# Three pieces of a recurrence's element-wise work change engine: GpSimd's subtractions to VectorE, its copies to ScalarE

## The chip, the cores and the metric

The kernel runs on one core of a Trainium2 chip. The time is the device time of one execution in microseconds (us), the median of three runs. Engines are named as in the profile: PE is TensorE (its weight loads are PEld), DVE is VectorE, ACT is ScalarE, POOL is GpSimd, and SP is the engine that issues the transfers.

## The reference, cut to what matters

One decoder layer over 1024 tokens of width 1024, in float32:

```
h  = rmsnorm(x);  u = h @ w_in            # 1024 x 5376, split into the parts below
oA = RWKV7(u[:, :1792])                   # 8 heads of 64, state 64x64, one step per token
oB = DiffAttention(u[:, 1792:3328])       # 4 heads, two softmax maps each
x += (sig(gA) * (oA @ PA) + sig(gB) * (oB @ PB)) @ w_out
x += relu(rmsnorm(x) @ W1)^2 @ W2
x += (p @ w_ple) * sig(rmsnorm(x) @ w_ple_gate)
out = rmsnorm(x)

S_t = S_{t-1} diag(w_t) + (S_{t-1} a_t) b_t^T + v_t k_t^T ;  y_t = S_t r_t
y   = groupnorm(y) * lnx_w + lnx_b ;  oA = (y + bonus) * g
```

## The kernel before, in words

Every large product is made from three products of split operands: a value is stored as `hi` (its rounding to a shorter format) and `lo` (what the rounding left), and `mm3` (L155 to L160) adds hi·hi (L158), hi·lo (L159) and lo·hi (L160). So each weight tile needs one cast for `hi` (ACT, L151) and one subtraction for `lo` (L152). `weights` (L143) issues the transfer of the raw tile on SP (L148), the cast, and the subtraction on POOL or DVE, by its argument `lo`.

The first phase, 40 to 700 us, holds the projection with `w_in` and the recurrence together. The projection is a generator, `stream`: 42 jobs of 128 output columns, each two halves of 24 matmuls of 512 columns, and each `next(stream)` issues three matmuls. Raw weights have one buffer, hi and lo two each, so the cast of job n+1 waits until PE has finished with job n-1, and the transfer of a raw tile waits until the subtraction before it has read the buffer. The halves land in two PSUM buffers (`pd`) and are emptied by `spill` (L330 to L347) or `mixed` (L305 to L311), on ACT and DVE.

The recurrence runs in four passes of two heads (`rwkv`). A pass prepares decays, keys and bonus (L403 to L471, on ACT, DVE and PE; `vs` is the value tile with the two 64-token halves of each block swapped, L460); forms small triangular matrices (L496 to L510); inverts them on DVE in 31 dependent steps of two instructions (L525, L526), with transfers through DRAM before (`dr_blk`) and after (`dr_inv`, `XS`); and then runs 18 ticks in which units of 128 tokens are built (L618 to L645) and the state is carried forward (L605 on PE, L609 on DVE). A group norm over four units runs beside the ticks (L585 to L597, with POOL's power of -1/2 at L107), and `post` forms the branch's output `of`, its hi part (L670) and its lo part (L671), and stores both. Between these steps the passes call `next(stream)` a fixed number of times, so that PE has projection work while the other engines work on the chain.

Each engine takes its instructions in one fixed order. That order is written when the kernel is built, by a planner that goes through the program in order of priority and places what it expects to be ready; so it is near the order of the text, not the same (L378 stands before L375 on DVE). An instruction that waits holds all that is behind it on its engine. On SP, transfers are issued in the same manner.

Of the kernel before, what the change touches and what calls it, by code (L numbers as in the profile page):

```python
# [10 lines left out]
F32R = mybir.dt.float32r  # L11
BF16 = mybir.dt.bfloat16
AF = mybir.ActivationFunctionType
ALU = mybir.AluOpType
# [4 lines left out]
P = 128  # L19
# [3 lines left out]
KD = D // P  # L23
# [56 lines left out]
class Kern:  # L80
# [82 lines left out]
    def run(self):  # L163
        nc, tc, A = self.nc, self.tc, self.A
        with ExitStack() as es:
# [24 lines left out]
            with ExitStack() as right:  # L190
                mA = self.phase_a2(opener, right, a1r, stream)
                front.close()
                mid = ExitStack()
                self.f1w = opener(mid)("f1w", 5)

                hb = opener(mid)("hb", 1)
                self.hb = {i: [hb.tile([P, 4, H], F32R, name=f"hb{i}{n}") for n in ("hi", "lo")] for i in (0, 1)}
                self.h2 = opener(mid)("h2", 1).tile([P, KD, T], F32, name="h2")
                with ExitStack() as e:
                    self.out_proj(opener(e), mA)  # L200
# [12 lines left out]
    def phase_a1(self, pool, rpool):  # L213
# [16 lines left out]
        with tc.tile_pool(name="a1n", bufs=2) as nw:  # L230
            def scale(j):

                sq = nw.tile([P, D], BF16, tag="sq", name="sq")
                ss = nw.tile([P, 1], F32, tag="nrm_ss", name="nrm_ss")
                nc.scalar.activation(sq, xs[j], AF.Square, accum_out=ss)
                r = self.rstd(nw, ss, 1, 1.0 / D, NORM_EPS)
                d = nw.tile([P, P], F32, tag="diag", name="diag")
                nc.vector.tensor_scalar(d, self.cst("ident"), r, None, op0=ALU.mult)
                return d

            xs = []
            for j in range(NT):
                xs.append(nw.tile([P, D], F32, tag="xj", name="xj", bufs=6))
                nc.sync.dma_start(xs[j], A["x"][j * P:(j + 1) * P, :])
                if j == 0:
                    nc.sync.dma_start(self.cs, A["cst"])
                    nc.sync.dma_start(self.prm, A["prm"])
                if j == 3:
                    next(stream)
            diag = scale(0)  # L250
            for j in range(NT):
                turn, diag = diag, scale(j + 1) if j + 1 < NT else None
                for _ in range(EARLY[j]):
                    next(stream)
                self.norm_turn(xs[j], "norm_mix_g", [t[:, :, j * P:(j + 1) * P] for t in hT], (nw, nw, self.ps), turn, nc.gpsimd)
# [13 lines left out]
    def stream(self, jobs):  # L269

        nc = self.nc
        load = lambda n, lo="g": self.weights(self.wp, self.A["w_in"][jobs[n][1]], [P, KD, P], "w", lo=lo, raw_bufs=1)

        order = [(n, c, c + 256) for c in (0, 256) for n in range(2)] + [(n, H, T) for n in range(2)]
        order += [(n, c, c + H) for n in range(2, len(jobs)) for c in (0, H)]
        w, pts, dst = {0: load(0, "v"), 1: load(1, "v")}, {}, {}
        yield
        for n, c0, c1 in order:
            if c0 == H and n and n + 1 < len(jobs):
                w[n + 1] = load(n + 1)  # L280
            kind, ct = jobs[n]
            wh, wl = w[n]
            if c0 % H == 0:
                pts[n] = self.pd.tile([P, H], F32, tag="pd", name="pd")
            pt = pts[n][:, c0 % H:(c1 - 1) % H + 1]
            for k in range(KD):
                self.mm3(pt, wh[:, k, :], wl[:, k, :], self.hT[0][:, k, c0:c1], self.hT[1][:, k, c0:c1], k == 0, k == KD - 1)
                if k + 1 < KD:
                    yield
            if c1 % H == 0:  # L290
                half, cols = c0 // H, slice(c1 - H, c1)
                if kind == "out":
                    self.spill(ct - 14, half, cols, pts[n])
                else:
                    dst[n] = self.mixed(kind, ct, half, cols, pts[n], dst.get(n))
            yield
# [98 lines left out]
    def rwkv(self, hp, r, k, v):  # L395
        nc, f4, ps, sm = self.nc, self.f4, self.ps, self.sm
# [51 lines left out]
        v4 = lambda t: t.rearrange("p (j c t) -> p j c t", j=NT, c=2)  # L448
# [8 lines left out]
        yield PRE[4]  # L457
        vs = F("vs")
        for c in range(2):
            nc.gpsimd.tensor_copy(v4(vs)[:, :, c, :], v4(v)[:, :, 1 - c, :])  # L460
        bv = F("bv")
        rkh = f4.tile([P, T], F32R, tag="f4", name=f"rkh_{hp}")
        nc.scalar.copy(rkh, rk)
# [58 lines left out]
        for s in range(31):  # L522
            n, m = s + 1, 31 - s
# [17 lines left out]
        for n in range(2):  # L541
# [4 lines left out]
            for c, b in enumerate(tops):  # L546
                dst = self.Tbd[b, :, blk[2 * c + 1]] if n else O[b]
# [8 lines left out]
        for tick in range(2 * NT + 2):  # L556
# [7 lines left out]
            if 0 <= j < NT:  # L564
                n = 2 * j + stage
# [83 lines left out]
    def post(self, hp, Y, norm, bv, F, PS, halves):  # L649

        nc = self.nc
        sgd = F("sgd")
        nc.sync.dma_start(sgd, self.dr_gd)
        of = F("of")
        for _ in norm:
            pass
        for q, c in enumerate(halves):
            yield POST[q]
            py = PS()
            for j in range(4):  # L660
                self.transpose(py[:, j * P:(j + 1) * P], Y[:, 4 * q + j, :])
            o = of[:, c]
            nc.scalar.activation(o, py, AF.Identity, bias=self.par("lnx_b", hp), scale=self.par("lnx_w", hp))
            nc.vector.tensor_tensor(o, o, bv[:, c], op=ALU.add)
            pg = PS()
            nc.tensor.matmul(pg, self.g2[:, hp * P:(hp + 1) * P], sgd[:, c], start=True, stop=True)
            nc.vector.tensor_tensor(o, o, pg, op=ALU.mult)

            hi = sgd[:, c].bitcast(F32R)
            nc.scalar.copy(hi, o)  # L670
            nc.gpsimd.tensor_tensor(o.bitcast(F32R), o, sgd[:, c], op=ALU.subtract)  # L671
            nc.sync.dma_start(self.dr_oa[hp, 0, :, c], sgd[:, c])
            nc.sync.dma_start(self.dr_oa[hp, 1, :, c], o)

# [584 lines left out]
```

## Time and profile before

| | |
|---|---|
| median of three runs | 1812.93 us (1809.47 to 1815.60) |
| the profiled execution | 1816.31 us, span 1814.5 us |
| granted PE clock over the span | 0.989 of full speed |
| busy share of the span | PE 96%, PEld 79%, DVE 57%, ACT 35%, POOL 28% |
| the phase with the change | 40 to 700 us |

A time in the text counts from the start of the span of the profiled execution. The granted clock has two levels, 1.0 (2.4 GHz) and 0.5 (1.2 GHz); a value between is a mean over a stretch.

### The profile page before, as it was taken

To read this page: it belongs to the slowest core of one execution; us is meant where nothing else is said; L and a number is where in the kernel's file an instruction comes from. 1 tells how busy PE (TensorE), PEld (TensorE's weight loads), DVE (VectorE), ACT (ScalarE), POOL (GpSimd) and SP (SyncE) were. 2 spreads that over 40 slices of the span, in tenths; PEclk is the share of its full clock that TensorE was granted. 3 is DMA by queue.
4 is the path that set the end of the run, shared out by engine and by line. 5 is a ranking of instruction groups with operands and counts; after the bars stand their busy time and mean duration, and the time that the engine had idled before them with its cause. 6 is when DMAs were issued, how large, how long until landed. Compare 5 with 4: busy or idle time off the path is not lost. (4 is left out here: it accounts for less than half of the span.)

```text
span 1814.5 us, 24028 instructions
## 1 busy us (share of the span) xinstructions
PE 1749.5 (96%) x9002; PEld 1433.6 (79%) x9002; DVE 1028.6 (57%) x2003; ACT 626.2 (35%) x1188; POOL 502.7 (28%) x377
## 2 busy tenths in 40 slices
PE   7999999999999999999999999999999999999998
PEld 7778777777777887788787778888878888888787
DVE  6257575667656652867646896666633333332653
ACT  4231442253253252867323422222231111112432
POOL 4221122122213121101512133333355333334000
PEclk9999999999999999999999999999999999999999
DMA  4323312311222327851553233333284222203101
GB/s 163 88 70 107 91 59 77 87 47 53 73 71 85 93 77 192 249 158 48 185 177 106 91 129 121 110 108 107 93 308 162 93 93 93 93 24 116 47 36 47
DMA packets 98276, 191.66 MB, mean 106 GB/s; under 512 B 34032, under 2 KB 35056, under 8 KB 98160
## 3 DMA queue, kind: packets, MB, share of 16 engines
q1 hardware_dynamic: 98160, 190.13, 32.6%
q8 instruction: 71, 1.16, 0.3%
q14 instruction: 45, 0.37, 0.1%
HBM read 138.19 MB, written 51.90 MB: 105 GB/s over the span
## 5 line engine op out<-in xcount | busy, mean ns | idle before, releaser
L158 PE MATMUL pd<-hT,w_hi 128*128 128x512 f32 (+1 forms) x688 | 276.9, 402 | 8.3 <-DVE edge L309 3.9
L160 PE MATMUL pd<-hT,w_lo 128*128 128x512 f32 (+1 forms) x688 | 270.9, 394 | 0.3 <-DVE w_lo L152 0.3
L159 PE MATMUL pd<-hT,w_hi 128*128 128x512 f32 (+1 forms) x688 | 271.0, 394 | 0.0
L1120 DVE TENSOR_TENSOR x<-x,p 128x1024 f32<-128x1024 f32 x64 | 78.2, 1221 | 209.1 <-PE p L160 209.1
L152 POOL TENSOR_TENSOR w_lo<-w_raw,w_hi 128x1024 fp32r<-128x1024 f32 x40 | 97.1, 2428 | 294.5 <-ACT w_hi L151 294.5
L158 PEld LDWEIGHTS pd<-hT,w_hi 128*128 128x128 f32 x688 | 131.1, 191 | 34.7 <-issue 5.5
L160 PEld LDWEIGHTS pd<-hT,w_lo 128*128 128x128 f32 x688 | 131.0, 190 | 24.7 <-DVE w_lo L152 0.5
L159 PEld LDWEIGHTS pd<-hT,w_hi 128*128 128x128 f32 x688 | 131.1, 191 | 23.8 <-issue 1.4
L953 POOL TENSOR_TENSOR wlo<-s,whi 128x512 fp32r<-128x512 f32 x56 | 74.9, 1340 | 186.3 <-ACT whi L952 186.3
L952 ACT CAST whi<-s 128x512 fp32r<-128x512 f32 x64 | 39.5, 622 | 120.9 <-PE p L159 101.8
L151 ACT CAST w_hi<-w_raw 128x1024 fp32r<-128x1024 f32 x42 | 44.1, 1050 | 92.7 <-PE pd L159 82.2
L952 ACT CAST h0hi<-h0r 128x1024 fp32r<-128x1024 f32 x8 | 8.4, 1053 | 190.3 <-PE p L159 181.4
L525 DVE TENSOR_TENSOR XT<-X,LB 64x31 f32<-64x31 f32 (+15 forms) x124 | 53.6, 432 | 22.2 <-DMA LB<-dr_blk 18.3
L839 DVE CUSTOM_DVE_ANT_0 sc<-ps,tab 128x512 f32<-128x512 f32 (+3 forms) x96 | 50.6, 551 | 25.4 <-PE ps L837 24.9
L953 POOL TENSOR_TENSOR h0lo<-h0r,h0hi 128x1024 fp32r<-128x1024 f32 x8 | 19.3, 2414 | 159.8 <-ACT h0hi L952 159.8
L1031 DVE SCALAR_TENSOR_TENSOR o<-x 128x512 f32<-128x512 f32 x52 | 61.9, 1190 | 0.7
L306 DVE SCALAR_TENSOR_TENSOR mix<-pd,prm,mix 128x511 f32<-128x511 f32 x28 | 20.9, 747 | 69.2 <-ACT mix L305 69.0
L877 POOL TENSOR_TENSOR r<-e,mhalf 128x1 f32<-128x1 f32 x32 | 19.8, 620 | 140.3 <-DVE e L875 131.0
L952 ACT CAST whi<-w_raw 128x512 fp32r<-128x512 f32 x48 | 29.7, 623 | 83.0 <-PE p L159 77.9
L107 POOL TENSOR_TENSOR rs_r<-rs_v,mhalf 128x1 f32<-128x1 f32 (+1 forms) x32 | 28.9, 903 | 91.8 <-DVE rs_v L105 91.8
L526 DVE TENSOR_TENSOR X<-X,XT 64x31 f32<-64x31 f32 (+15 forms) x124 | 52.0, 419 | 4.1
L848 ACT ACTIVATE sc<-sc,nm 128x128 f32<-128x128 f32 (+7 forms) x64 | 49.5, 776 | 11.8 <-DVE nm L846 7.2
(416 smaller groups left out, 4699.5 us busy)
## 6 DMA issues: line engine op xcount, KB each, us to landing
w_raw<-w_in SPq DMA_DIRECT2D x42, 512.0 KB, 3.4
w_raw<-w_ff SPq DMA_DIRECT2D x36, 512.0 KB, 3.8
dr_hid<-o SPq DMA_DIRECT2D x64, 256.0 KB, 2.1
dr_gate<-st SPq DMA_DIRECT2D x32, 256.0 KB, 2.3
gate<-dr_gate SPq DMA_DIRECT2D x32, 256.0 KB, 2.8
xj<-x SPq DMA_DIRECT2D x8, 512.0 KB, 6.1
qs<-dr_q SPq DMA_DIRECT2D x8, 512.0 KB, 8.2
kh<-dr_k SPq DMA_DIRECT2D x16, 256.0 KB, 9.1
```

Source lines behind the costliest of these rows:

```text
L152: (nc.gpsimd if lo == "g" else nc.vector).tensor_tensor(lo_, raw, hi_.bitcast(F32), op=ALU.subtract)
L158: mm(out, wh, hh, start=first, stop=False, skip_group_check=more)
L159: mm(out, wh, hl, start=False, stop=False, skip_group_check=more)
L160: mm(out, wl, hh, start=False, stop=last, skip_group_check=more)
L525: nc.vector.tensor_tensor(t, X[:, 0:n, s:s + 1].to_broadcast([64, n, m]), LB[:, s:s + 1, s + 1:].to_broadcast([64, n, m]), op=ALU.mult)
L526: nc.vector.tensor_tensor(X[:, 0:n, s + 1:], X[:, 0:n, s + 1:], t, op=ALU.add)
L839: nc.vector.tensor_tensor_reduce(s[:, c0:c1], pss[:, 0:c1 - c0], tab[:, o + c0:o + c1], 1.0, NEG, op0=ALU.add, op1=ALU.max, accum_out=mx[: ...
L848: nc.scalar.activation(s[:, 0:kend], s[:, 0:kend], AF.Exp, bias=nm, scale=SLOPES[h], accum_out=t)
L952: self.nc.scalar.copy(hi, src)
L953: (self.nc.vector if on_vector else self.nc.gpsimd).tensor_tensor(lo, src, hi.bitcast(F32), op=ALU.subtract)
L1031: nc.vector.scalar_tensor_tensor(o, src, 0.0, src, op0=ALU.max, op1=ALU.mult)
L1120: nc.vector.tensor_tensor(self.x2[:, j, :], self.x2[:, j, :], pt, op=ALU.add)
```

## The change

Three places in the first phase change engine; shapes, data and the order of the text stay. The subtraction for `lo` in `stream` goes from POOL to DVE for jobs 2 to 41 (jobs 0 and 1 were on DVE already); the two copies that make `vs` in each pass go from POOL to ACT; and the subtraction for the lo part of the branch's output in `post` goes from POOL to DVE, two in each pass.

```diff
 def stream(self, jobs):
-        load = lambda n, lo="g": self.weights(self.wp, self.A["w_in"][jobs[n][1]], [P, KD, P], "w", lo=lo, raw_bufs=1)
+        load = lambda n: self.weights(self.wp, self.A["w_in"][jobs[n][1]], [P, KD, P], "w", lo="v", raw_bufs=1)
...
-        w, pts, dst = {0: load(0, "v"), 1: load(1, "v")}, {}, {}
+        w, pts, dst = {0: load(0), 1: load(1)}, {}, {}
...
 def rwkv(self, hp, r, k, v):
         for c in range(2):
-            nc.gpsimd.tensor_copy(v4(vs)[:, :, c, :], v4(v)[:, :, 1 - c, :])
+            nc.scalar.copy(v4(vs)[:, :, c, :], v4(v)[:, :, 1 - c, :])
...
 def post(self, hp, Y, norm, bv, F, PS, halves):
             nc.scalar.copy(hi, o)
-            nc.gpsimd.tensor_tensor(o.bitcast(F32R), o, sgd[:, c], op=ALU.subtract)
+            nc.vector.tensor_tensor(o.bitcast(F32R), o, sgd[:, c], op=ALU.subtract)
```

## Rows read from the trace of the kernel before

**Rows 1.** The page, part 1: busy time, share and instructions of each engine.

```profile
PE 1749.5 (96%) x9002; PEld 1433.6 (79%) x9002; DVE 1028.6 (57%) x2003; ACT 626.2 (35%) x1188; POOL 502.7 (28%) x377
```

**Rows 2.** Windows: length, busy PE, PEld, DVE, ACT, POOL, clock, DMA share, GB/s.

```profile
40.00:700.00 660.00, 633.69 (x3719) 511.61 (x3718) 397.64 (x897) 235.29 (x444) 167.25 (x149) 0.98 0.27 80
```

**Rows 3.** The four stretches of that phase with a lowered clock; columns as above.

```profile
120.00:140.00 20.00, 18.11 (x91) 13.69 (x90) 15.38 (x21) 4.47 (x7) 7.80 (x7) 0.91 0.45 107
230.00:250.00 20.00, 16.59 (x84) 13.54 (x83) 13.43 (x33) 9.59 (x24) 5.79 (x5) 0.83 0.11 36
330.00:350.00 20.00, 16.11 (x59) 12.73 (x58) 12.98 (x35) 4.40 (x4) 2.41 (x1) 0.83 0.30 68
420.00:440.00 20.00, 17.28 (x88) 13.37 (x87) 14.34 (x20) 3.56 (x6) 8.56 (x8) 0.91 0.12 39
```

**Rows 4.** Waits of PE, 40 to 700 us: us in total, times, longest.

```profile
PE ps L468 <- ACT rkh L463: 5.9, 3, 2.7
PE pd L158 <- DVE edge L309: 3.9, 1, 3.9
PE pyg L605 <- DVE MS L609: 3.3, 1, 3.3
PE pd L158 <- DVE stlo L333: 3.1, 2, 1.6
PE ps L642 <- ACT GY L645: 3.1, 3, 1.7
PE pw L545 <- DMA XS<-dr_inv: 2.9, 3, 1.6
PE ps L469 <- DVE rkl L465: 1.9, 1, 1.9
```

**Rows 5.** Two lines of DVE: ns min/median/max, first and last start.

```profile
L311 DVE TENSOR_TENSOR mix<-mix,edge x14: 142/1194/1217, 66.6 to 478.1; 128x1 f32<-128x1 f32 x14
...
L643 DVE TENSOR_TENSOR GY<-ps,RA x64: 405/422/429, 212.0 to 678.0; 64x256 f32<-64x256 f32 x64
```

**Rows 6.** Timeline of DVE, the last instruction held by a POOL subtraction: start, length.

```profile
624.99 2.40 DVE L525 TENSOR_TENSOR XT<-X,LB 64x156 f32<-64x156 f32 x1
```

**Rows 7.** Timeline, 233 to 239 us, the ticks of pass 0.

```profile
233.07 1.66 POOL L107 TENSOR_TENSOR rs_r<-rs_v,mhalf 128x8 f32<-128x8 f32 x1 [0.68 <-DVE rs_v L105]
...
234.69 2.35 POOL L152 TENSOR_TENSOR w_lo<-w_raw,w_hi 128x1024 fp32r<-128x1024 f32 x1
234.76 2.83 DVE L597 TENSOR_TENSOR Y<-Y,rs_r 128x512 f32<-128x512 f32 x1 [1.53 <-POOL rs_r L107]
...
238.42 0.69 PE L605 MATMUL pyg<-MS,GY 128*128 128x64 f32 x2 [3.33 <-DVE MS L609]
```

**Rows 8.** Instructions that write w_lo; columns as in 5.

```profile
L152 POOL TENSOR_TENSOR w_lo<-w_raw,w_hi x40: 2347/2397/3240, 47.0 to 697.7; 128x1024 fp32r<-128x1024 f32 x40
L152 DVE TENSOR_TENSOR w_lo<-w_raw,w_hi x2: 1218/1222/1225, 13.0 to 23.1; 128x1024 fp32r<-128x1024 f32 x2
```

**Rows 9.** Instructions of single lines and tiles; columns as in 5.

```profile
L455 DVE SCALAR_TENSOR_TENSOR a<-mix,prm,a x4: 1272/1452/3422, 123.8 to 567.9; 128x1024 f32<-128x1024 f32 x4
...
L460 POOL COPY vs<-mix x8: 612/1606/1617, 119.3 to 568.4; 128x512 f32<-128x512 f32 x8
...
L670 ACT CAST sgd<-of x8: 619/620/622, 248.1 to 695.5; 128x512 fp32r<-128x512 f32 x8
```

**Rows 10.** Groups by line, 160 to 195 us, the inversion of pass 0.

```profile
L152 POOL TENSOR_TENSOR w_lo<-w_raw,w_hi 128x1024 fp32r<-128x1024 f32 x3 | 7.4, 2457 | 24.5 <-ACT w_hi L151 24.5
```

**Rows 11.** Timeline of DVE, the inversion of pass 1.

```profile
335.05 1.84 DVE L525 TENSOR_TENSOR XT<-X,LB 64x207 f32<-64x207 f32 x1
```

**Rows 12.** Waits of ACT, 40 to 700 us; columns as in 4.

```profile
ACT w_hi L151 <- PE pd L159: 82.2, 24, 5.8
```

**Rows 13.** Timeline of ACT, the preparation of pass 2.

```profile
426.95 1.04 ACT L463 CAST rkh<-rk 128x1024 fp32r<-128x1024 f32 x1 [6.19 <-DVE BK L454]
```

**Rows 14.** The same subtraction in the later projection, on DVE already.

```profile
L152 DVE TENSOR_TENSOR gw_lo<-gw_raw,gw_hi x16: 684/685/1775, 780.2 to 906.5; 128x512 fp32r<-128x512 f32 x16
```

## The prediction

> **What bounds the kernel now.** I read the busy shares first, then the windows, then the waits of PE, then the instructions of the tiles that the change names, then the timeline round each wait. The shares say PE: 96% of the span, with DVE at 57% and POOL at 28% [rows 1]. So an edit on DVE, ACT and POOL is worth what it takes from PE's idle time or gives back of its clock, and nothing else. The window of the changed phase shows what there is to take: of 660 us PE is busy 633.7, so it idles 26.3 us, and DVE is busy 397.6, that is 60% [rows 2]. Four stretches have a lowered clock: 0.91, 0.83, 0.83 and 0.91 over 20 us each, so (0.09 + 0.17 + 0.17 + 0.09) x 20 = 10.4 us of PE work is lost there [rows 3]. Each lies at one of PE's longer stalls: 1.9, 3.3, 3.9 and 2.7 us, ended by `rkl`, `MS`, `edge` and `rkh` [rows 4]. Idle time and clock together, 36.7 us or 2.0% of the span, are the most that any change in this phase can bring. About 1.6 us of it, a stall on `stlo` at 46 us, belongs to the setup ahead of the passes, and stays.
>
> The waits say who ends these stalls: nearly always DVE, or ACT behind DVE; no wait of PE in that list names POOL [rows 4]. POOL's 40 subtractions end early enough, so their length in itself costs nothing. What they do is seen on DVE. The one-column addition L311 takes 0.14 us alone and 1.19 to 1.22 us in more than half of its 14 runs; in the timeline each long one ends where a POOL subtraction ends, and this repeats through the phase, the last time at 625 us, where an inversion step that has the form of its 0.32 us neighbours takes 2.40 [rows 5, 6]. I count 26 DVE instructions so lengthened, and their excess adds up to some 46 us, near 2.1 us for each that meets a subtraction at its start. All read two SBUF tensors or copy within SBUF. L643, which takes one of its two inputs from PSUM, never does it: 64 runs between 0.405 and 0.429 us [rows 5]. So a POOL subtraction shuts such DVE work out for as long as it runs. The clearest stall is in the ticks of pass 0: L597 starts behind a POOL subtraction, takes 2.83 us, `MS` is queued behind it, and PE waits 3.33 us for `MS` [rows 7].
>
> **The subtractions on DVE.** Forty of 2.40 us leave POOL and forty of 1.22 us join DVE [rows 8]: DVE gets 40 x 1.22 = 48.8 us, and loses the 46 us of being shut out. Its sum hardly moves; what changes is where the time falls. A hold of 2.1 us becomes a piece of 1.22, 0.87 us less at each place where PE now waits behind one, and all of it where the planner puts the piece behind the urgent instruction. Stage by stage:
>
> Preparation. In a pass an instruction such as L455, 1.27 us alone, takes 3.42 [rows 9]; `rkh` and `rkl` come after, and PE waits 5.9 + 1.9 = 7.8 us for them over the four passes [rows 4]. The hold of 2.15 becomes 1.22: 4 x 0.93 = 3.7 less. Bounds: nothing, and all 7.8.
>
> Emptying PSUM during the inversion. PE waits 3.9 us for `edge` and, without the setup's 1.6, 1.5 us for `stlo` [rows 4]. Both stand in DVE's queue among inversion steps, and three subtractions fall into an inversion [rows 10]: 3 x 0.87 = 2.6 us sooner at the end of one. The last hold ahead of `edge` is a 1.84 us step just in front of it [rows 11]; a planner that counts the subtraction as DVE work can leave it behind `edge`. I take 3.0 of the 3.9 and all 1.5: 4.5. Bounds: nothing, and 5.4.
>
> Ticks. L597 would take its 0.69 with the 1.22 us piece done during the 1.66 us for which DVE waits on the power [rows 7]: 2.7 of the 3.3 us go. One wait for `GY` of 1.7 us in pass 1 stands behind a hold too: 0.9 less [rows 4]. Together 3.6. Bounds: nothing, and 6.4 (3.3 and 3.1).
>
> The end of the inversion. PE waits 2.9 us in three of four passes for `XS` [rows 4]. Inversions that are 2.6 us shorter would clear them. But PE also arrives sooner: in pass 1, where it does not wait today, by the 3.0 us above and the 3.4 us of clock, against 2.6. Something up to 3.8 us comes back there. I set the two against each other: 0.
>
> Clock. The four stalls that go with lowered clock shrink to about 0.9, 0.6, 0.9 and 1.8 us. Stalls of 1.5 to 1.7 us elsewhere in this phase (`stlo`, `GY`, `XS`) had none [rows 3, 4]. I count the 10.4 us as gone and give 1.8 back for a stall that moves to `XS` in pass 1: 8.6. Bounds: nothing, and 10.4.
>
> Fourteen subtractions hold nothing today, and on DVE they are new work: 14 x 1.22 = 17.1 us is the upper bound, 0 the lower. DVE is busy 60%, so some 10 us falls on queued work, and PE has projection matmuls to run meanwhile. I take 4.
>
> A transfer of raw weights is issued on SP once the subtraction has read the buffer; it is released 1.2 us sooner if DVE comes at once, and ACT has then mostly to wait for PE anyhow (24 casts, 82.2 us) [rows 12]. Nothing, as long as that cover of 3.4 us on average stands.
>
> **The copies on ACT.** Eight copies of 0.61 to 1.62 us leave POOL; ACT takes about 0.62 for a 128x512 copy within SBUF [rows 9], 8 x 0.62 = 5.0 us as upper bound. They stand ahead of `rkh`, and there ACT is idle: 6.2 us before `rkh` in pass 2, waiting for DVE [rows 13]. I take 0. Where ACT had no such wait, `rkh` would be 1.2 us later in a pass.
>
> **The branch's lo parts on DVE.** Eight subtractions of 128x512, 0.685 us each by the same work elsewhere [rows 14]: 5.5 us at most, 0 at least. They follow a cast on ACT at a pass's end, when DVE also begins the next preparation. I take 1.
>
> **The sum**: -3.7 - 4.5 - 3.6 + 0 - 8.6 + 4 + 0 + 1 = -15.4 us. The profiled execution took 1816.3, 3.4 above the median of the runs. It gives 1800.9 from the one and 1797.5 from the other; I say 1799.
>
> A rule of the skill would make more of it. The Trainium skill (GPSIMD Engine Reference, Engine selection) tells one to put two-input element-wise work on VectorE, about twice as fast as GpSimd. By the length of the instructions that would be 40 x (2.40 - 1.22) = 47 us; as no PE wait names POOL, and PE idles only 26, the sum does not use it.
>
> **The rivals.**
> *The stalls only move* (0.18). DVE's total is +48.8 + 5.5 - 46 = +8 us. If the chain through DVE (preparation, inversion, ticks) and not PE's queue sets the length of a pass, PE's stalls come back one stage later, at `XS` above all. For it: PE waits for that chain at each of its stages. Against: PE has no other idle time in 96% of the phase. Time: 1812.9 + 8 less half of the clock's 10.4, about 1816, between 1808 and 1818.
>
> *DVE waits in its queue* (0.15), the other side. A subtraction on DVE must wait for ACT's cast, and the cast waits for PE: 24 times, 3.4 us on average [rows 12]. On POOL nobody stood behind it. On DVE the inversion steps, `edge`, `stlo` and `MS` do. In the twelve subtractions of the inversions, 0.87 us of waiting each eats the shorter hold; the whole gain of 15.4 is gone at 0.87 + 15.4 / 12 = 2.2 us each; at 3.4 us it is 12 x 1.2 = 14 slower: 1827. For it: the casts of the inversions are the ones that wait. Against: the planner places a subtraction when it expects the cast to be done, and DVE's same subtraction later in the kernel has no idle time of its own [rows 14].
>
> *All of it* (0.12): every stall behind a hold goes, with the clock, and the new work is hidden: 24.7 + 10.4 = 35 less, 1778.
>
> *The moved piece is shut out itself* (0.05). It has two SBUF inputs, so POOL's remaining work can hold it as it held L597: the power of 1.66 us, which stood right ahead of a POOL subtraction in pass 0 [rows 7] and in two others. Three such holds: 5 us, 1804. The Trainium skill (GPSIMD Engine Reference, Specifications) says that GpSimd's SBUF interfaces are shared with VectorE, for instructions with two SBUF inputs or in a two-port mode. By that rule it would happen; rows 5 agree on which instructions are shut out.
>
> **How the numbers follow.** The forecast, a gain of 6 to 28 us, has 0.50; with the last two rivals, 0.67 is faster by over 0.3%. That bound, 5.4 us, is about what the spread of the runs can tell from no change. Same 0.18, slower 0.15. The range leaves out the far end of the full gain and of the queue's wait: 1783 to 1819. The likeliest case alone spans 1785 to 1807.
>
> **What would show it.** In the changed kernel, L311 at 0.14 to 0.15 us throughout, L455 near 1.27, no L525 over 0.5; `w_lo` on DVE at 1.22. PE's waits for `MS` and `edge` gone, those for `rkh` about halved, clock at 1.0 in three of the four stretches. The copies on ACT at 0.62, with `rkh` not later. Wrong if DVE's waits list `w_lo` behind `w_hi` with more than 20 us, if waits for `XS` grow beyond 8 us, or if the planner's new order makes PE wait in places that have no wait today.

## The result, and the profile after

The changed kernel takes 1786.01 us (median of four runs, 1782.61 to 1786.95) against 1811.96 us for four runs of the kernel before in the same session: a ratio of 0.9854, with a 95% interval of 0.9842 to 0.9867. It is 26 us faster; the forecast was 14. The direction and the range held, the size did not: the true gain is nearly twice the sum.

The profiled execution took 1785.2 us with a span of 1783.5, against 1816.3 and 1814.5: 31 us apart, 5 more than the medians, because the profiled run of before was a long one: its clock was 0.989 over the span, where most other runs of that kernel have 0.991 or 0.992, and 0.002 of the span is 3.6 us. The account below is made on these two executions.

First the busy shares. DVE's total moved from 1028.6 to 1031.8 us, as forecast, and POOL lost 114 us [rows 1].

```profile
PE 1735.6 (97%) x9002; PEld 1424.3 (80%) x9002; DVE 1031.8 (58%) x2051; ACT 631.0 (35%) x1196; POOL 388.9 (22%) x321
```

Then the windows of the changed phase: the whole phase, and the four stretches that had a lowered clock [rows 2, 3].

```profile
40.00:700.00 660.00, 650.45 (x3846) 526.98 (x3845) 406.57 (x987) 249.09 (x479) 53.03 (x94) 1.00 0.31 91
120.00:140.00 20.00, 19.87 (x116) 15.42 (x116) 16.86 (x32) 6.04 (x10) 4.26 (x6) 1.00 0.43 106
230.00:250.00 20.00, 18.44 (x103) 15.08 (x103) 15.18 (x38) 10.80 (x25) 3.88 (x4) 1.00 0.15 53
330.00:350.00 20.00, 19.85 (x209) 15.30 (x207) 6.54 (x13) 7.60 (x14) 0.00 (x0) 1.00 0.39 80
420.00:440.00 20.00, 20.00 (x118) 16.41 (x118) 10.91 (x33) 5.39 (x8) 0.00 (x0) 1.00 0.22 54
```

PE idles 9.5 us of 660 where it idled 26.3, and the granted clock is 1.00 in all four stretches. The first matmul of the phase behind (L836) starts at 682.4 us instead of 710.4, so 28 of the 31 us come from here. The other 3 lie later; added up over windows of 10 us from 700 us on, the time lost to a lowered clock fell from 8.6 to 4.4 us.

The waits of PE in the same phase (us in total, times, longest):

```profile
PE ps L99 <- DVE Y L597: 4.4, 3, 1.5
PE pd L158 <- DVE stlo L333: 1.6, 1, 1.6
PE ps L468 <- ACT rkh L463: 0.8, 1, 0.8
PE ps L642 <- ACT XV L632: 0.6, 2, 0.3
...
PE pyg L605 <- DVE MS L609: 0.3, 1, 0.3
```

Of the waits of before [rows 4], those for `edge`, `XS`, `rkl` and `GY` are gone, not smaller; `rkh` fell from 5.9 to 0.8 and `MS` from 3.3 to 0.3; `stlo` keeps the 1.6 us of the setup. One wait is new: L597, at the end of a pass, for the normalised `Y`.

The lines that the forecast named, in ns (min/median/max), with first and last start:

```profile
L311 DVE TENSOR_TENSOR mix<-mix,edge x14: 142/149/160, 67.6 to 453.5; 128x1 f32<-128x1 f32 x14
L455 DVE SCALAR_TENSOR_TENSOR a<-mix,prm,a x4: 1272/1276/1280, 124.2 to 542.0; 128x1024 f32<-128x1024 f32 x4
L152 DVE TENSOR_TENSOR w_lo<-w_raw,w_hi x42: 1209/1224/1226, 13.9 to 670.7; 128x1024 fp32r<-128x1024 f32 x42
L460 ACT COPY vs<-mix x8: 608/620/632, 120.1 to 541.2; 128x512 f32<-128x512 f32 x8
```

L311 no longer has a long run, L455 is back at 1.27 us [rows 5, 9], and no subtraction on DVE is longer than 1.23 us, so none is itself shut out. Before, 34 DVE instructions of the phase are held, by 50.6 us in all: 26 of them, with 46.5 us, behind the stream's subtractions, the other eight behind POOL's copies (L460) and its subtractions in `post` (L671). The last is L597 at 687 us, not the inversion step of [rows 6].

What this does to a chain is clearest in the preparation of pass 2. In the timeline of before, around [rows 13]:

```profile
419.25 1.23 DVE L442 TENSOR_TENSOR k<-k,mix 128x1024 f32<-128x1024 f32 x1
420.34 2.39 POOL L152 TENSOR_TENSOR w_lo<-w_raw,w_hi 128x1024 fp32r<-128x1024 f32 x1 [9.57 <-ACT w_hi L151]
420.39 3.42 DVE L455 SCALAR_TENSOR_TENSOR a<-mix,prm,a 128x1024 f32<-128x1024 f32 x1
422.67 3.16 POOL L460 COPY vs<-mix 128x512 f32<-128x512 f32 x2
423.74 1.63 DVE L445 SCALAR_TENSOR_TENSOR rk<-mix,prm,k 128x1024 f32<-128x1024 f32 x1
425.29 1.63 DVE L454 TENSOR_TENSOR BK<-k,Wi 128x1024 f32<-128x1024 f32 x1
```

The same steps in the timeline of the changed kernel:

```profile
401.44 1.16 DVE L442 TENSOR_TENSOR k<-k,mix 128x1024 f32<-128x1024 f32 x1
402.52 1.27 DVE L455 SCALAR_TENSOR_TENSOR a<-mix,prm,a 128x1024 f32<-128x1024 f32 x1
403.71 1.28 DVE L445 SCALAR_TENSOR_TENSOR rk<-mix,prm,k 128x1024 f32<-128x1024 f32 x1
404.90 1.22 DVE L454 TENSOR_TENSOR BK<-k,Wi 128x1024 f32<-128x1024 f32 x1
406.04 1.22 DVE L456 TENSOR_TENSOR BK<-a,Wi 128x1024 f32<-128x1024 f32 x1
406.16 1.05 ACT L463 CAST rkh<-rk 128x1024 fp32r<-128x1024 f32 x1 [1.96 <-DVE BK L454]
407.17 1.22 DVE L152 TENSOR_TENSOR w_lo<-w_raw,w_hi 128x1024 fp32r<-128x1024 f32 x1
408.31 1.22 DVE L465 TENSOR_TENSOR rkl<-rk,rkh 128x1024 fp32r<-128x1024 f32 x1
```

Before, the subtraction on POOL began just ahead of L455 and held it for 2.15 us, and the copies on POOL lengthened L445 and L454 by some 0.4 us each. After, the subtraction is DVE's own instruction and stands *behind* L454 and L456, in the time in which ACT makes `rkh`. The chain to `rkh` has no piece of 1.22 us in the place of the hold: it has nothing there. The cast starts 4.7 us after L442 instead of 7.7.

### The profile page after: what moved, and what is told of

Same layout as the page of the kernel before. It is cut to its first block, busy times and chain, and to the rows that moved or that the text cites. A ratio compares the mean times of both kernels' runs of the same rounds, so it can differ in the third digit from the quotient of the medians.

```text
span 1783.5 us, 24054 instructions
## 1 busy us (share of the span) xinstructions
PE 1735.6 (97%) x9002; PEld 1424.3 (80%) x9002; DVE 1031.8 (58%) x2051; ACT 631.0 (35%) x1196; POOL 388.9 (22%) x321
## 5 line engine op out<-in xcount | busy, mean ns | idle before, releaser
L628 POOL COPY XV<-vt 64x128 f32<-64x128 f32 x64 | 21.0, 328 | 461.9 <-PE ps L642 365.5
L152 DVE TENSOR_TENSOR w_lo<-w_raw,w_hi 128x1024 fp32r<-128x1024 f32 x42 | 51.3, 1221 | 72.3 <-ACT w_hi L151 71.9
L159 PE MATMUL po<-wo_lo,mh 128*128 128x512 f32 x128 | 50.2, 393 | 2.4 <-POOL wo_lo L152 2.2
L159 PE MATMUL p<-w1lo,h1hi 128*128 128x512 f32 x128 | 49.9, 390 | 1.1 <-DVE w1lo L953 1.1
```

What stands on the lines that cost most here:

```text
L152: (nc.gpsimd if lo == "g" else nc.vector).tensor_tensor(lo_, raw, hi_.bitcast(F32), op=ALU.subtract)
L159: mm(out, wh, hl, start=False, stop=False, skip_group_check=more)
```

## The experiments

The theory after this reading: POOL's subtractions cost what they did by shutting DVE out; once they are DVE's own, DVE's work falls into gaps of its chains, so nearly the whole hold goes. The rivals: the gain comes from the new order of the instructions on PE (by pass, 14, 11, 10 and 8 more projection matmuls stand ahead of the first `XS` matmul), or from the two small parts, or a piece does replace each hold and something else gave the rest.

**Each part alone.** Three kernels, each the kernel before with one part of the change:

```diff
-        w, pts, dst = {0: load(0, "v"), 1: load(1, "v")}, {}, {}          # e1: every load with lo="v"
+        w, pts, dst = {0: load(0), 1: load(1)}, {}, {}
...
-            nc.gpsimd.tensor_copy(v4(vs)[:, :, c, :], v4(v)[:, :, 1 - c, :])   # e2
+            nc.scalar.copy(v4(vs)[:, :, c, :], v4(v)[:, :, 1 - c, :])
...
-            nc.gpsimd.tensor_tensor(o.bitcast(F32R), o, sgd[:, c], op=ALU.subtract)   # e3
+            nc.vector.tensor_tensor(o.bitcast(F32R), o, sgd[:, c], op=ALU.subtract)
```

> Only the subtractions of the stream go to DVE; the vs copies and the branch's lo parts stay on POOL. Theory 'holds' (the POOL subtractions shut DVE's two-input work out, and that is nearly all): 21 to 27 us faster than before, ratio 0.985 to 0.989, L311 at 0.15 us, no L525 over 0.5 us. Rival 'the small parts carry a share' (the copies on ACT let rkh start sooner): 10 to 18 us faster, and PE still waits over 3 us for rkh.

> Only the vs copies go to ACT. 'Holds': the copies hold DVE for some 2 us in all, so 0 to 4 us faster, ratio 0.998 to 1.000. Rival 'the small parts carry a share': 6 to 12 us faster. ACT's queue as a new cost: up to 5 us slower.

> Only the branch's lo parts go to DVE. 'Holds': three DVE instructions are held for under 2 us in all, against 5.5 us of new DVE work: within 3 us of before, ratio 0.998 to 1.002. Rival 'the small parts carry a share': 5 us or more faster.

Measured: e1 1786.11 us (0.9856, 0.9841 to 0.9871), e2 1808.13 (0.9972, 0.9963 to 0.9982), e3 1809.38 (0.9985, 0.9976 to 0.9994), against 1812.39 for the kernel before. The stream's subtractions carry the whole gain. The small parts are worth 4.3 and 3.0 us by themselves, at the upper end of what was expected of them or just above it, and 0.1 us on top of e1: the stalls that they shorten, `rkh` among them (5.9 to 4.4 in e2 and in e3), are gone already there, as PE's waits in e1 show:

```profile
PE ps L99 <- DVE Y L597: 3.1, 2, 1.6
PE pd L158 <- DVE stlo L333: 1.6, 1, 1.6
PE ps L468 <- ACT rkh L463: 1.5, 2, 1.3
```

**The shutting out alone, put back.** The changed kernel, where POOL does the same subtraction as well, into a tile that nobody reads:

```diff
         (nc.gpsimd if lo == "g" else nc.vector).tensor_tensor(lo_, raw, hi_.bitcast(F32), op=ALU.subtract)
+        if tag == "w" and self.junk is not None:
+            nc.gpsimd.tensor_tensor(self.junk, raw, hi_.bitcast(F32), op=ALU.subtract)
...
+        self.junk = one.tile([P, KD, P], BF16, name="junk")
```

> The changed kernel with the POOL subtraction put back beside DVE's, into a scratch tile that nobody reads: the engines' queues keep the work of the changed kernel, and only the shutting out comes back. 'Holds': 15 to 35 us slower than the changed kernel, 1800 to 1822, L525 again up to 2.5 us, PE waits for edge, MS or rkh again. 'The planner's order alone': within 5 us of the changed kernel.

Measured: 1830.09 us (1.0086 of before, 1.0052 to 1.0120), so 44 us more than the changed kernel's 1786.01 of the other session, and 42 by the two ratios to before; more than the 15 to 35 expected. PE's instructions stand in the order of the changed kernel, to the projection matmul ahead of each `rkl` and each `XS`. The waits are back. Its phase in a window, and PE's waits there (its line numbers are 1 to 5 higher):

```profile
40.00:700.00 660.00, 624.16 (x3646) 500.92 (x3645) 444.05 (x928) 236.32 (x446) 166.50 (x128) 0.98 0.25 76
```

```profile
PE ps L100 <- DVE Y L602: 8.4, 3, 3.0
PE ps L473 <- ACT rkh L468: 5.2, 3, 3.0
PE pd L161 <- DVE stlo L337: 4.7, 3, 2.1
PE pd L161 <- DVE edge L313: 4.2, 1, 4.2
PE pw L550 <- DMA XS<-dr_inv: 3.7, 2, 3.5
PE ps L474 <- DVE rkl L470: 2.9, 1, 2.9
PE pd L161 <- DVE mix L310: 2.7, 1, 2.7
PE pyg L610 <- DVE MS L614: 2.5, 3, 1.1
```

Six of the seven waits of [rows 4] are among them, from the same lines of the program; `GY` (3.1 us before) is not, L597 has come, and `mix` has grown from 0.8 to 2.7 us. I count some 30 DVE instructions lengthened against others of their line and form, by about 54 us in all (34 and 50.6 us before, none after). PE idles 35.8 us against 9.5, and lowered clock costs 15.3 us against none: 41.6 us, near the difference of the two spans (40.8). So the order of the changed kernel is not what gained; the same order loses all of it to the holds. The 44 us are not the price of the holds as they were before, though: here POOL's subtraction starts beside DVE's own, takes 3.34 us in the median where it took 2.40, and five of the lengthened instructions are DVE's own subtractions. POOL's copy of the work also keeps the raw buffer longer, but no wait of PE names a transfer of weights or the cast behind it.

**No subtraction at all.** The kernel before, in which jobs 2 to 41 use the lo parts of jobs 0 and 1 again; the forty subtractions are left out of the computation:

```diff
+        if not isinstance(lo, str):
+            nc.scalar.copy(hi_, raw)
+            return hi_, lo
...
-                w[n + 1] = load(n + 1)
+                w[n + 1] = load(n + 1, w[(n + 1) % 2][1])
```

> The kernel before with the subtractions of the stream's jobs 2 to 41 left out altogether (those jobs use the lo parts of jobs 0 and 1, so the projection's lo-hi products are not those of the reference); nothing else moves. It has the order that the planner writes without DVE work for the subtraction, and no holds by it. Theory 'holds': DVE has 49 us less than in the changed kernel and is never shut out for long, so as fast or faster, 1776 to 1787. Theory 'order' (the changed kernel gains because the planner, which sees the subtraction in DVE's queue, puts more projection matmuls ahead of the waiting ones): the order is that of before, PE waits for XS and rkh remain over 5 us in all, 1790 to 1802.

Measured: 1781.91 us (0.9834, 0.9822 to 0.9847), 30.8 less than the 1812.66 of before in its session. PE's projection matmuls ahead of each `rkl` and `XS` are those of before within two, so here the order is not changed and the holds are gone: five are left in the phase, 2.5 us in all. PE's waits in the phase:

```profile
PE pd L161 <- DVE stlo L336: 1.6, 1, 1.6
PE ps L645 <- ACT GY L648: 1.3, 2, 0.7
PE pyg L608 <- DVE MS L612: 1.1, 1, 1.1
```

There is none for `edge`, `rkl` or `XS`. This prices both halves of the change: to lose the forty subtractions on POOL is worth 30.8 us, and to do them on DVE costs 1786.0 - 1781.9 = 4.1 us, for 48.8 us of work. The 4.1 is a difference of two sessions; the gains over before, each in its own session, put it at 30.8 - 26.3 = 4.5 us (e1, which leaves the small parts on POOL as e9 does), and by their intervals it is uncertain by some 3 us. A raw buffer is free sooner here too, but no wait of PE in the kernel before names a transfer of weights or a cast of them.

**More of DVE's work.** The changed kernel with each stream subtraction done a second time (e4), and with half of it done twice (e11):

```diff
-        (nc.gpsimd if lo == "g" else nc.vector).tensor_tensor(lo_, raw, hi_.bitcast(F32), op=ALU.subtract)    # e4
+        for _ in range(2 if tag == "w" else 1):
+            (nc.gpsimd if lo == "g" else nc.vector).tensor_tensor(lo_, raw, hi_.bitcast(F32), op=ALU.subtract)
...
+        if tag == "w":                                                     # e11
+            nc.vector.tensor_tensor(lo_[:, 0:4, :], raw[:, 0:4, :], hi_[:, 0:4, :].bitcast(F32), op=ALU.subtract)
```

> The changed kernel with each subtraction of the stream done twice on DVE (same result), so that a job takes 2.44 us of DVE, as long as POOL's subtraction shut it out before. Theory 'size' (the gain is 1.2 us instead of 2.4 at each place): the gain is lost, 1808 to 1816. Theory 'placement' (work that stands in DVE's own queue is put where nothing urgent waits, whereas a hold falls on whatever comes): most of the gain stays, 1788 to 1796.

> The changed kernel with half of each subtraction of the stream done a second time on DVE (0.69 us more per job, same result). Done twice in full it cost 19.7 us, of which a stretch of 20.5 us at half clock explains 10. If the rest grows with the work: 1789 to 1793 with the clock at 1.0 round 140 us. If the work is free up to a point: 1785 to 1788. If the clock falls there as well: 1798 to 1803.

Measured: e4 1805.67 us (0.9960, 0.9948 to 0.9973), between its two forecasts and in neither, e11 1806.62 (0.9956, 0.9934 to 0.9977), above all three of its own. That looks like a price on DVE's work, but half of the work should then cost half. The windows tell otherwise. PE's idle time in the phase is 14.2 us in e4 and 10.1 in e11, against 9.5. What e4 has is a long stretch at half clock; windows of 5 us there:

```profile
130.00:135.00 5.00, 4.00 (x32) 3.02 (x31) 4.89 (x8) 1.18 (x2) 2.91 (x3) 1.00 0.28 59
135.00:140.00 5.00, 5.00 (x20) 3.90 (x19) 2.71 (x10) 0.54 (x1) 0.00 (x0) 0.59 0.52 150
145.00:150.00 5.00, 5.00 (x22) 3.67 (x23) 2.99 (x10) 0.58 (x1) 0.00 (x0) 0.50 0.01 2
155.00:160.00 5.00, 5.00 (x24) 4.18 (x24) 0.15 (x1) 0.74 (x2) 0.00 (x0) 0.86 0.31 52
```

With a short stretch at 426 us, lowered clock costs e4 12.0 us; with the idle time that is 16.7 of its 19.7 us, and the rest is not accounted for. The profiled run of e11 has two such stretches, of 20.5 us each, at 280 and at 427 us; a window inside each:

```profile
285.00:290.00 5.00, 5.00 (x25) 3.78 (x25) 2.66 (x9) 0.58 (x1) 0.00 (x0) 0.50 0.14 52
435.00:440.00 5.00, 5.00 (x19) 3.56 (x16) 2.99 (x10) 2.19 (x3) 0.00 (x0) 0.50 0.00 0
```

That is 2 x 20.5 x 0.5 = 20.5 us, its whole loss. Its twelve runs go with their granted clock over the span: 1785.95 us at 0.997, 1796.4 at 0.991, 1799.9 at 0.989, and the other nine, 1806.3 to 1809.1, at 0.981 to 0.986. From the first to the second, 0.006 of the span is 10.7 us, and the times are 10.4 apart. So the clock makes the difference between the runs; how many stretches each had is shown for the profiled run alone. The run at 0.997 takes what the changed kernel takes, with 28 us more of DVE's work in it. In the profiled runs those 28 us cost 0.6 us of PE's idle time, and 49 us more cost 4.7. But the work is not free of the clock: all five runs of e4 (0.989 to 0.990) and eleven of the twelve of e11 lost some, against 0.994 to 0.998 in the four of the changed kernel. That more work on DVE brings these stretches about, by longer stalls of PE in the small triangular products, fits the profiles and is not shown.

**The holds in pieces.** The kernel before, POOL's subtraction in four of 256 columns, so that DVE can begin between two of them:

```diff
+        if tag == "w" and lo == "g":
+            for q in range(4):
+                s = slice(2 * q, 2 * q + 2)
+                nc.gpsimd.tensor_tensor(lo_[:, s, :], raw[:, s, :], hi_[:, s, :].bitcast(F32), op=ALU.subtract)
+            return hi_, lo_
```

> The kernel before with each POOL subtraction of the stream cut into four of 256 columns; nothing else moves. 'Holds': a DVE instruction is shut out for one piece (0.7 to 0.8 us) instead of 2.1, if DVE gets in between two pieces: L311 at most 0.8 us, 12 to 25 us faster than before. If POOL keeps the interface from piece to piece: L311 stays near 1.2 us, and the time within 5 us of before. Theory 'the planner's order alone' (POOL's work is not in DVE's queue, so DVE's order is that of before): no gain even if the holds shrink.

Measured: 1810.34 us (0.9972, 0.9953 to 0.9991). That is 3.6 us faster, not the 12 to 25 expected; by its time alone this run would speak for the planner's order. The holds did shrink: none is over 0.62 us, the excess sums to about 30 us where it was 50.6 (there are twice as many), and PE idles 18.8 us instead of 26.3. But lowered clock costs 15.3 us instead of 10.2, one stretch of 20.5 us at 137 us in it, and takes most of that back. So this run does not decide between the theories; e6 and e9 do.

**The new wait.** Four kernels tried to get the 4.4 us at L597 back: by another number of projection steps ahead of the two halves of `post` (e7, e10), and with a copy of the setup on ACT, to shorten its `stlo` (e8 on e7, e12 on e10):

```diff
-PRE, INV, SUB, UN, POST = [2, 4, 4, 2, 4, 2], 28, 4, 3, [4, 17]
+PRE, INV, SUB, UN, POST = [2, 4, 4, 2, 4, 2], 28, 4, 3, [7, 14]      # e7, e8;  e10, e12: [4, 20]
...
-        nc.vector.tensor_copy(self.RA[:, :, 2, :, :].rearrange("p j c t -> p j (c t)"),
+        nc.scalar.copy(self.RA[:, :, 2, :, :].rearrange("p j c t -> p j (c t)"),      # e8, e12
```

> The changed kernel with three more steps of the projection ahead of the transposes in post (7 and 14 instead of 4 and 17), against its one new wait, PE for the last group norm (L597, 4.4 us in three passes). If that wait is on the path: 3 to 5 us faster than the changed kernel, 1781 to 1783. If it moves to another wait of the pass's end: the same within 2 us.

> The same, and the copy that fills the constant part of RA at the setup (L378, 3.5 us on DVE, shut out by POOL's memsets) goes to ACT, which is idle then. 'Holds': the stall of 1.6 us on stlo at 47 us goes, 1 to 2 us faster than without. Rival: ACT's copy makes sthi late instead, no change.

> The changed kernel with three more steps of the projection (2.0 us of PE) ahead of the second half's transposes in post (20 instead of 17), which wait for the last group norm, 4.4 us in three passes. If that wait is on the path: 2 to 4 us faster than the changed kernel, 1782 to 1784. If it turns up elsewhere: 1785 to 1787.

> The same with the setup's copy into RA on ACT: 0 to 1.5 us less again, 1781 to 1784.

Measured: 1785.59, 1785.01, 1785.92 and 1786.51 us; none stands clear of the changed kernel. The setup's `stlo` falls from 1.6 to 1.1 us in e8 and e12. e7 leaves the wait at 4.4. e10 halves it, and PE then waits at the head of the next phase, as its waits show:

```profile
PE ps L836 <- DMA kh<-dr_k: 3.9, 1, 3.9
PE ps L99 <- DVE Y L597: 2.0, 2, 1.5
```

The 2.4 us saved come back as 3.9 us for a transfer. No version that beats both kernels came out of this.

## Why the forecast had the direction right and the size wrong

The mechanism stood: POOL's subtraction shuts out DVE's work within SBUF, and PE's stalls stood behind that. The step that failed is a size: "A hold of 2.1 us becomes a piece of 1.22, 0.87 us less at each place where PE now waits behind one". The same sentence names the case that came true, "all of it where the planner puts the piece behind the urgent instruction", but the sum takes it in part only (`edge`, `stlo`, L597), and not in the preparation. Each of the gains came out larger than its term, the preparation by 3.3 us, `XS` (set to 0) by 2.9, the ticks and the emptying by about 2 each, the clock by 1.8. Term by term, on the profiled pair:

| term | forecast | measured |
|---|---|---|
| preparation (`rkh`, `rkl`) | -3.7 | 7.8 to 0.8: -7.0 |
| emptying PSUM (`edge`, `stlo`; also `mix`, `st`) | -4.5 | 6.6 to 0: -6.6 |
| ticks (`MS`, `GY`, `XV`) | -3.6 | 6.9 to 1.1: -5.8 |
| `XS` | 0 | 2.9 to 0: -2.9 |
| lowered clock in the phase | -8.6 | 10.4 to 0: -10.4 |
| new work on DVE (+4) and `post` (+1) | +5 | new wait at L597: +4.4 |
| sum | -15.4 | -28.3 |

The phase ended 28.0 us sooner in this pair; the medians are 26 us apart.

- *Preparation.* Over passes 1 to 3 the time from `k` on ACT (L441) to the cast of `rkh` fell by 2.2, 2.6 and 1.4 us, on average 2.1: a whole hold, where 0.93 was taken. In pass 0 it grew by 0.5: the hold stood behind that cast there (L456 at 125 us), in front of `rkl`, whose wait of 1.9 us went. The upper bound in the text, all 7.8, was near the truth.
- *Emptying and inversion.* Inside an inversion the sized step held: the piece stands among the steps there, and the inversions, from their first step to their last, became 1.3, 3.2, 2.2 and 3.3 us shorter, 2.5 on average against 2.6 forecast. But the waits at `edge` and `stlo` went altogether, since those instructions no longer stood behind a hold. `mix` and `st` were not in the sum (1.2 us).
- *`XS`.* The gain of the inversions and PE's earlier arrival were set against each other. In the changed kernel 8 to 14 more projection matmuls stand ahead of `XS`, some 0.23 us of PE from one start to the next, 1.8 to 3.2 us in all, and cover the arrival. They are not needed for it: e9, with the order of before, has no wait for `XS`, and e6, with the order of after, has 3.7 us.
- *Clock.* It followed the stalls; the 1.8 us given back for a stall at `XS` were not lost.
- *New work.* This term was about right: +4 forecast for the stream, 4 to 4.5 by e9.
- *Copies and `post`.* 0 and +1 forecast; in the whole change they are worth nothing that can be measured. That they are faster alone (e2, e3) was not foreseen: on POOL they too hold DVE, eight times (4 us) in the phase.

The rivals. "The stalls only move" fell: no stage took over a stall but L597. "DVE waits in its queue" fell, although its marker came true: DVE's waits list `w_lo` behind `w_hi` with 71.9 us, 20 times, where more than 20 us was to mean the forecast wrong. Many of them lie where DVE has only the projection's work, at 50 to 115 us. Two stand ahead of an inversion and do delay it, the 11.3 us at 302 and this one, in pass 3:

```profile
572.00 0.47 SPq L516 DMA_DIRECT2D LB<-dr_blk  x1
577.08 1.23 DVE L152 TENSOR_TENSOR w_lo<-w_raw,w_hi 128x1024 fp32r<-128x1024 f32 x1 [8.51 <-ACT w_hi L151]
578.40 0.18 DVE L525 TENSOR_TENSOR XT<-X,LB 64x31 f32<-64x31 f32 x1
```

The first step starts 6.4 us after the transfer of `LB` is issued; in the kernel before and in e9 it is 3.7 us in this pass. So the queue's wait cost the inversion 2.7 us here, and 1.3 in pass 1 (6.7 against 5.4). No wait of PE for `XS` came of it, because the inversions are shorter and more projection matmuls stand ahead. It was a bad marker: a wait costs only if something urgent stands behind it and PE has nothing else to run. Another sign of being wrong came true as well: PE waits at a place that had no wait, L597, for 4.4 us. It is what the new work costs. "All of it", at 1778, was nearest: its benefit is there (e9, 30.8 against 35), and only its free new work is not. "The moved piece is shut out itself" did not occur: no piece over 1.23 us.

The Trainium skill (GPSIMD Engine Reference, Specifications) says that GpSimd's SBUF interfaces are shared with VectorE. The runs agree and add the price: with POOL's subtraction back beside DVE's own, about 54 us of holds and 44 us of time (e6). The Trainium skill's rule that VectorE does such work about twice as fast (GPSIMD Engine Reference, Engine selection) agrees with the trace in the lengths, 2.40 and 1.22 us. It gave 47 us in the forecast's aside and points the right way for another reason: without the subtraction at all the kernel gains 30.8, so no speed of it can be worth more here.

Left open: what decides in a run whether a stretch of 20.5 us at half clock occurs, which moves the time of e4, e5 and e11 by 10 or 20 us, and why a hold costs more in the order of the changed kernel (44 us with it put back) than in that of before (30.8 with it taken out).

## What to carry to other kernels

An instruction that another engine can hold is late by the whole hold, at a place that no planner of the order knows; when the holder's work moves onto the held engine's own queue, the order sees it and can put it behind what is urgent, so price the hold at its full length and the moved work by the engine's free time, as two terms. Price each by its own run: one with the work left out, one with the hold alone put back. Judge a wait in a queue by what stands behind it in the timeline, not by its sum.

## What the runs showed of the hardware

The clock stayed at half (0.50, 1.2 GHz) for 20.5 us at a time in e4, e5 and e11, while the profile shows PE busy 5.00 of every 5.00 us (the windows of e4 and e11 above). Each time it fell where PE runs the small triangular products (L496 to L510), after a stall for `AKx` of 1.0 us in e4, 1.8 in e5, 0.5 and 0.7 in e11, and came back after the projection's matmuls had taken over again. The changed kernel runs through the same steps at 1.00, with 0.1 us of such a stall. One such stretch costs 10 us, more than any stall that came before it.

Between POOL's pieces of 256 columns (0.74 us each, e5) DVE gets in: the longest hold is 0.62 us where that behind a whole subtraction is 2.1 to 2.3. So the hold lasts one POOL instruction, not POOL's queue. It works the other way too: a piece of 0.74 us takes up to 1.77 us, and the subtraction of 2.40 us took 3.24 at 273 us in the kernel before, where a DVE instruction with two SBUF inputs (L445) was running when it started.
